# Loads that wait for values, sums begun sooner, and odd chunks on column groups of their own, in a hybrid decoder layer

## The chip, the cores and the metric

The kernel runs on one core of a Trainium2 chip. The time is device microseconds (us) of one execution; a kernel is timed in several runs and the median is taken. One further execution is recorded by the hardware profiler; its trace gives the start and the length of every instruction on TensorE (PE, and PEld for its weight loads), VectorE (DVE), ScalarE (ACT), GpSimd (POOL), on the queue of SyncE (SP), and of every DMA.

## The reference

One decoder layer on x of 1024 tokens by 1024 channels, all in float32:

- h = rmsnorm(x, norm_g) * (1 + scale) + shift, with scale, shift and gate from silu(c) @ w_ada + b_ada
- proj = h @ w_in, cut into q_a, k_a, v_a, z_a (512 wide each: 8 heads of 64) and q_b, f_b, i_b, z_b, g_a, g_b (1024 wide each)
- attention on q_a, k_a, v_a: three dilated causal windows (128 by 1, 512 by 4, 2048 by 16) with a bias by distance, merged by their softmax denominators, then times silu(z_a)
- a gated recurrence on q_b, f_b, i_b, 8 heads of key width 128 and value width 128:

```python
f = lb + (1 - lb) * sigmoid(f_b);  k = 1 - f
S_t = diag(f_t) S_{t-1} + k_t i_t^T;   o_t = S_t^T silu(q_t)
```

- the recurrence's output is normalised and multiplied by silu(z_b); y = sigmoid(g_a) * (o_a @ w_branch_a) + sigmoid(g_b) * (o_b @ w_branch_b)
- out = rmsnorm(x + gate * (y @ w_out), final_g)

## The kernel before

**Products.** A float32 operand is split into a high and a low part (`split`, L243: the high part is a cast on ACT, the low part a subtraction on DVE, helper `sub` at L224). A product of 128 x 128 weights with 128 x 512 of h is then three matmuls (`mm3`, L238 to L241: low times high, high times low, high times high). h is kept transposed as four blocks b11, b12, b21, b22 (halves of the channels by halves of the tokens). Pairs of 128-column units of w_in share their products in Strassen's manner (`add_pair`, L265): seven products on b11, b21, b22 and on the block differences t1 = b12 - b11, t3 = b22 - b12, t2 = b22 - t1, t4 = b21 - t2, instead of eight. The differences are built in place in the tiles xt, by `block_sum` (L667): for each name and each half c of the rows one subtraction on DVE, one cast on ACT (t1h and so on) and one subtraction on DVE (t1l and so on).

**The stream.** All weight products stand in one list of steps (`Stream`, L71). A step's weights are prepared two steps ahead. Raw weight tiles (w_raw) are loaded through SyncE's queue (L258) as soon as a tile of the ring is free; from the thirteenth on, the ring has tiles that take the memory of the start, xt among it. `Filler` (L168) runs pieces of the stream, a group of three matmuls each, between other work: `fill(amount)` owes `amount * rate` groups, about 3.6 for one unit in attention. What leaves PSUM goes through six buffers named ct (`ctile`, L262): products kept for later (L327), and results on their way to DRAM, whose buffer is free again when the write has landed.

**The start (to about 110 us).** x is normalised and turned, h is made block by block (`make_h`, `turn_late`), and the first three units (columns of q, k and v of the first head pair) run along with it (`first_products`, into the banks pm). PE's order is written out by hand in the whole kernel; in the start that of ACT, DVE and GpSimd is too. Between these steps stand calls of `tick` (L680): each begins one more block sum, if one is left, and takes one step of each sum under way.

**Attention (about 110 to 470 us).** For each head, `load_head` (L867) loads the first halves (512 tokens) of q (qp), and of the high and low parts of k (k1, k2), by six loads of 128 KB (`load_half`, L886), a Toeplitz tile of biases (toep, 512 KB, L877) and the values of the first half (`load_value`, vq, L891). All of these go through GpSimd's queue and come from DRAM, where `ev_split` (L428, L429) and the transposes of `ev_v` (L453, vq_d) have put them. The score of 128 queries (`score`, L893) is two matmuls into the bank pss, a sum with toep and a running minimum on DVE (L906), an exp on ACT and two operations on DVE; `turn` (L914) transposes it, and `value` (L929) multiplies it with the values. `begin` (L948) yields after each of the two scores of an item (a head and 256 queries); after the second block of queries (i = 1) it has the second halves and their values loaded, after the last (i = 7) the next head. From the end of the start on, a planner orders the instructions of all engines but PE, loads among them, by when it expects their operands: a load may be issued ahead of its place in the source. So the second halves of head 0 are issued from 89.56 us on, ahead of its first values at 102.11 us.

**The recurrence (about 550 to 950 us).** Each head's 1024 tokens are eight chunks of 128. Within a chunk the decayed products of k and q are built level by level (`recurrence`, L1081): at level hl, blocks of hl keys with the hl queries after them, for hl = 1, 2, 4, 8, 16 by full 32 x 32 tiles (`small`, L1094: output partitions 0, 32, 64 and 96 in turn, so four column groups of the array), for hl = 32 by sixteen products of 32 keys (L1113) and for hl = 64 by eight products of 64 keys (L1122). The output partitions of a matmul are the columns of the array that it uses. ACT copies the results of the last two levels into the matrix am (L1116, L1124), which is needed after all levels. Between the levels DVE updates k and q (L1126, L1128), and the filler runs stream steps.

After 950 us come the branch sums, the output product and the last norm.

Of the kernel before, what the change touches and what calls it, by code (L numbers as in the profile page):

```python
# [10 lines left out]
F32 = mybir.dt.float32  # L11
# [8 lines left out]
P = 128  # L20
S = 1024
# [158 lines left out]
def hybrid_layer(ctx: ExitStack, tc: tile.TileContext, x, w_ada, b_ada, w_in, w_branch_a, w_branch_b, w_out,  # L180
# [203 lines left out]
    def half_of(th):  # L384
        return slice(512 * th, 512 * th + 512)
# [129 lines left out]
    with ExitStack() as st:  # L515
# [113 lines left out]
        def turn_late(j):  # L629

            ps = px.tile([P, 512], F32, name="pxt")
            for t in range(4):
                nc.tensor.transpose(ps[:, t * P:t * P + P], xs[4 + t][:, j * P:(j + 1) * P], ident)
            make_h(j, 1, ps)
# [20 lines left out]
        def first_products(j, ths=(0, 1), us=(0, 1, 2)):  # L655
            for th in ths:
                bh, bl = X[NAMES[j // 4, th]]
                k = j % 4
                for u in us:
                    hi, lo = firsts[u + 3 * (j // 4)]  # L660
                    nc.tensor.matmul(main[u, th], hi[:, k], bh[:, k], start=j == 0, stop=False)
                    nc.tensor.matmul(main[u, th], lo[:, k], bh[:, k], start=False, stop=False)
                for u in us:
                    nc.tensor.matmul(main[u, th], firsts[u + 3 * (j // 4)][0][:, k], bl[:, k], start=False,
                                     stop=j == KT - 1)
# [8 lines left out]
            return [lambda: nc.vector.tensor_tensor(to, a, b_, ALU.subtract),  # L674
                    lambda: nc.scalar.copy(hi[:, s], to), lambda: sub(lo[:, s], to, hi[:, s])]

        sums = [(name, c) for name in ("t1", "t3", "t2", "t4") for c in range(2)]
        under_way = []

        def tick():  # L680

            if sums:
                under_way.append(block_sum(*sums.pop(0)))
            for parts in under_way:
                parts.pop(0)()
            while under_way and not under_way[0]:
                under_way.pop(0)
# [106 lines left out]
        first_products(2, (1,))  # L794
        tick()
        turn_late(3)
        first_products(3, (0,))
        mod_rows(2)
        first_products(3, (1,), (0,))
        mod_turn(2)  # L800
        for n in range(3, 6):
            split_first(n)
        first_products(3, (1,), (1,))
        mod_rows(3)
        first_products(3, (1,), (2,))
        mod_turn(3)
        tick()
        lx.close()
        add_blocks(hctx.enter_context(tc.tile_pool(name="hpool2", bufs=1, reuse_waits="tile")),
                   "b21", "b22", "t2", "t3")  # L810
        stream.issue()
        make_h(4, 0)
        turn_late(4)
        make_h(5, 0)
        first_products(4, (0,))
        turn_late(5)
# [42 lines left out]
    with ExitStack() as at:  # L859
# [7 lines left out]
        def load_head(h):  # L867
            p = h // 2
            if p > 0:
                stream.need(f"qk{p}")  # L870
            while turned.get(("v", p)) != 2:
                stream.step()
            qp, k1, k2 = ([ap1.tile([P, 512], F32R, name=f"{n}{c}") for c in range(2)] for n in ("qp", "k1", "k2"))
            toep = ap1.tile([P, S], F32, name="toep")
            heads[h] = qp, k1, k2, toep, [None, None]
            load_half(h, 0)
            nc.gpsimd.dma_start(toep, bass.AP(tensor=toep_d.tensor, offset=toep_d.offset + h * TOEP,  # L877
                                              ap=[[1, P], [1, S]]))
            load_value(h, 0)

        def load_half(h, c):
            qp, k1, k2, _, _ = heads[h]
            p, r = h // 2, slice(E * (h % 2), E * (h % 2) + E)
            for dst, n in ((qp, 4 * p), (k1, 4 * p + 2), (k2, 4 * p + 3)):
                for hh in range(2):
                    nc.gpsimd.dma_start(dst[c][E * hh:E * hh + E],  # L886
                                        qk_d[n + hh if dst is qp else n][r, half_of(c)].bitcast(F32R))
# [78 lines left out]
                value(*late.pop(0))  # L966

        load_head(0)
        fill.limit = in_gating
        fill.rate = (in_attention - stream.at) * 4 / NH / sum((j + 1) * w for j, w in enumerate(ATT_W))  # L970
        fill(2.0)
        for _ in begin(0):
            fill(0.5)
        for n, (h, j) in enumerate(items):
            nxt = begin(n + 1)
            for m in range(j + 1):
# [61 lines left out]
    with ExitStack() as hg:  # L1038
# [39 lines left out]
        def c3(t):  # L1078
            return t.rearrange("p (c t) -> p c t", c=8)

        def recurrence(h):  # L1081
# [17 lines left out]
            while hl < P:  # L1099
                q4 = qq.rearrange("p (n two t) -> p n two t", two=2, t=hl)  # L1100
                k4 = kk.rearrange("p (n two t) -> p n two t", two=2, t=hl)
                t3 = fq[:, :2 * n].rearrange("p (n two) -> p n two", two=2)
                if hl <= 16:
                    pl = small(2 if hl == 1 else 1)
                    if hl == 1:
                        nc.vector.tensor_tensor(d3, pl[:, :, 0], mask(0), ALU.mult)
                    nc.vector.copy_predicated(d3, mask(1 + LEVELS.index(hl)).bitcast(I32), pl[:, :, 1 if hl == 1 else 0])
                elif hl == 32:
                    pl = pp.tile([P, 512], F32, name="pp")[:, :256]
                    for c in range(8):  # L1110
                        for b in range(2):
                            o = c * P + 64 * b
                            nc.tensor.matmul(pl[64 * b:64 * b + 32, c * 32:c * 32 + 32], kk[:, o:o + 32],  # L1113
                                             qq[:, o + 32:o + 64], start=True, stop=True)
                    for b in range(2):
                        nc.scalar.copy(am[64 * b:64 * b + 32, :, 64 * b + 32:64 * b + 64],  # L1116
                                       c3(pl[64 * b:64 * b + 32]))
                else:
                    pl = pp.tile([P, 512], F32, name="pp")
                    for c in range(8):  # L1120
                        o = c * P
                        nc.tensor.matmul(pl[0:64, c * 64:c * 64 + 64], kk[:, o:o + 64], qq[:, o + 64:o + P],  # L1122
                                         start=True, stop=True)
                    nc.scalar.copy(am[0:64, :, 64:P], c3(pl[0:64]))  # L1124
                k_end = t3[:, :, 1:2].to_broadcast([P, n, hl])
                nc.vector.tensor_tensor(k4[:, :, 0, :], k4[:, :, 0, :], k_end, ALU.mult)  # L1126
                q_end = t3[:, :, 0:1].to_broadcast([P, n, hl])
                nc.vector.tensor_tensor(q4[:, :, 1, :], q4[:, :, 1, :], q_end, ALU.mult)  # L1128
                if fq is tot:
                    tn = g1.tile([P, S // 2], F32, name="totn")  # L1130
                    other = tot, tn
                else:
                    tn = other[0] if fq is other[1] else other[1]
                nc.vector.tensor_tensor(tn[:, :n], t3[:, :, 0], t3[:, :, 1], ALU.mult)
                fq = tn
                n //= 2
                hl *= 2
                yield 2.6
                if hl == 8:
                    load_z(h)  # L1140
                if hl == 32 and h + 1 < NHB:
                    load_f(h + 1)
# [317 lines left out]
```

## Time and profile before

| | |
|---|---|
| three runs | 1139.42, 1141.77, 1144.51 us; median 1141.77 us |
| the profiled execution | 1141.97 us, its span 1140.2 us |
| busy in the span: PE | 1112.2 us (98%), 8322 matmuls |
| PEld | 912.8 us (80%) |
| DVE | 808.2 us (71%) |
| ACT | 516.5 us (45%) |
| POOL | 117.2 us (10%) |
| DMA | 189.54 MB, mean 166 GB/s |
| granted TensorE clock, mean | 0.994 |

The span runs from the first to the last instruction. "Idle before" in a row is the time for which the engine stood still ahead of that instruction, with the instruction or DMA whose end released it. A matmul's end is modelled, and the next one starts before it; the time that a run of matmuls takes is therefore read from start to start.

### The profile page before, as it was taken

Reading aid. Unit: us, or ns where it says so; the run is one execution under the profiler, and the core shown is the slowest. Engines: PE = TensorE matmul, PEld = TensorE weight load, DVE = VectorE, ACT = ScalarE, POOL = GpSimd, SP = SyncE. Lnnn points to the kernel's source line nnn. Section 1 sums busy time; section 2 is a strip of 40 time slices with the busy share of each in tenths; the row PEclk is TensorE's granted clock in tenths of the full one; section 3 lists DMA queues with packets and bytes.
Section 4 is the critical chain, followed back from the end, with each engine's and each line's share of the span. In section 5 each row is a group of like instructions: output and inputs, shape, how many; then the busy total and the mean of one; then the engine's idle time right before and its main releaser. Section 6 shows DMA issues by size and latency. Waiting matters only on the chain.

```text
span 1140.2 us, 21715 instructions
## 1 busy us (share of the span) xinstructions
PE 1112.2 (98%) x8322; PEld 912.8 (80%) x8322; DVE 808.2 (71%) x1607; ACT 516.5 (45%) x1056; POOL 117.2 (10%) x195
## 2 busy tenths in 40 slices
PE   7998999999999999999999999999999999999997
PEld 5677788888888888878887878787887878888886
DVE  4486888878877776844778797878888773769053
ACT  4474555677555555632343444333443432334021
POOL 1102112202202201100000000000000012000000
PEclk9999999999999999999999999999999999999999
DMA  9739476656646624856625254443535379864052
GB/s 321 219 102 252 136 195 181 180 131 163 153 120 162 158 80 139 265 174 195 222 89 173 93 168 140 141 155 107 174 90 181 106 252 328 276 209 140 21 184 74
DMA packets 161480, 189.54 MB, mean 166 GB/s; under 512 B 11312, under 2 KB 107696, under 8 KB 161376
## 3 DMA queue, kind: packets, MB, share of 16 engines
q1 hardware_dynamic: 140080, 153.95, 42.3%
q0 software_dynamic: 20896, 33.60, 12.2%
q8 instruction: 65, 1.06, 0.4%
q10 hardware_dynamic: 400, 0.61, 0.2%
q14 instruction: 39, 0.32, 0.1%
HBM read 129.36 MB, written 58.76 MB: 165 GB/s over the span
## 4 chain that ended last, share of the span: by engine, by line
PE 85%; DVE 6%; DMA 4%; issue 2%; ACT 2%; POOL 1%; SPq 0%; POOLq 0%; DVEq 0%; ACTq 0%
PE m L239 18%; PE m L241 17%; PE m L240 16%; PE pq L240 4%; PE pq L241 4%; PE pq L239 4%; PE po L936 3%; PE pt L921 3%; PE pp L1094 3%; PE pss L904 2%; PE pss L903 1%; PE pou L1177 1%; PE pou L1162 1%; PE pou L1179 1%; PE pxt L640 1%
## 5 line engine op out<-in xcount | busy, mean ns | idle before, releaser
L224 DVE TENSOR_TENSOR w_lo<-w_raw,w_hi 128x512 fp32r<-128x512 f32 x156 | 106.7, 687 | 54.1 <-ACT w_hi L246 48.6
L246 ACT CAST w_hi<-w_raw 128x512 fp32r<-128x512 f32 x146 | 90.5, 620 | 59.9 <-PE m L241 50.3
L327 ACT COPY ct<-m 128x512 f32<-128x512 f32 x90 | 52.6, 585 | 93.7 <-PE m L241 72.0
L246 ACT CAST w_hi<-w_s 128x512 fp32r<-128x512 f32 x90 | 55.9, 621 | 74.0 <-PE m L241 51.0
L274 DVE TENSOR_TENSOR ct<-m,ct 128x512 f32<-128x512 f32 x90 | 61.8, 686 | 26.5 <-PE m L241 26.1
L224 DVE TENSOR_TENSOR w_lo<-w_s,w_hi 128x512 fp32r<-128x512 f32 x90 | 61.8, 687 | 15.2 <-ACT w_hi L246 13.5
L909 ACT ACTIVATE s<-s,st 128x128 f32<-128x128 f32 (+3 forms) x64 | 49.8, 778 | 31.5 <-DVE st L906 31.4
L925 ACT CAST pth<-pt 128x512 fp32r<-128x512 f32 (+1 forms) x80 | 43.6, 544 | 36.5 <-PE pt L921 32.0
L224 DVE TENSOR_TENSOR ptl<-pt,pth 128x512 fp32r<-128x512 f32 (+1 forms) x80 | 50.5, 631 | 7.7 <-ACT pth L925 7.0
L239 PE MATMUL m<-t2h,w_hi 128*128 128x512 f32 x120 | 50.4, 420 | 4.2 <-ACT ct L327 4.2
L1185 POOL TENSOR_TENSOR ssh<-ssh,halfh 128x4 f32<-128x4 f32 x16 | 18.1, 1128 | 345.1 <-DVE ssh L1184 345.1
L239 PE MATMUL m<-b11h,w_hi 128*128 128x512 f32 x124 | 51.6, 416 | 0.0
L239 PE MATMUL m<-b21h,w_hi 128*128 128x512 f32 x124 | 51.2, 413 | 0.0
L239 PE MATMUL m<-b22h,w_hi 128*128 128x512 f32 x124 | 50.8, 410 | 0.0
L239 PE MATMUL m<-t1h,w_hi 128*128 128x512 f32 x120 | 50.3, 419 | 0.5 <-DVE ct L274 0.5
L239 PE MATMUL m<-t4h,w_hi 128*128 128x512 f32 x120 | 49.6, 414 | 0.4 <-DVE ct L274 0.4
L239 PE MATMUL m<-t3h,w_hi 128*128 128x512 f32 x120 | 49.6, 414 | 0.0
L241 PE MATMUL m<-b11l,w_hi 128*128 128x512 f32 x124 | 48.8, 394 | 0.0
L241 PE MATMUL m<-b21l,w_hi 128*128 128x512 f32 x124 | 48.7, 393 | 0.0
L241 PE MATMUL m<-b22l,w_hi 128*128 128x512 f32 x124 | 48.7, 393 | 0.0
L240 PE MATMUL m<-b11h,w_lo 128*128 128x512 f32 x124 | 48.5, 391 | 0.0
L240 PE MATMUL m<-b21h,w_lo 128*128 128x512 f32 x124 | 48.5, 391 | 0.0
(358 smaller groups left out, 3193.8 us busy)
## 6 DMA issues: line engine op xcount, KB each, us to landing
w_raw<-in_w_in_dram SPq DMA_DIRECT2D x128, 256.0 KB, 3.4
wa<-in_w_ada_dram SPq DMA_DIRECT2D x16, 512.0 KB, 8.9
qk_d<-ct SPq DMA_DIRECT2D x32, 256.0 KB, 3.5
k<-qk_d POOLq DMA_DIRECT2D x64, 128.0 KB, 4.9
qp<-qk_d POOLq DMA_DIRECT2D x32, 128.0 KB, 4.9
toep<-toep_d POOLq DMA_DIRECT2D x8, 512.0 KB, 6.5
vq_d<-ct SPq DMA_DIRECT2D x16, 256.0 KB, 3.4
vq<-vq_d POOLq DMA_DIRECT2D x16, 256.0 KB, 4.2
```

What stands on the lines that cost most here:

```text
L224: nc.vector.tensor_tensor(out_, a, hi.bitcast(F32), ALU.subtract)
L239: nc.tensor.matmul(ps, ah, bh, start=start, stop=False, skip_group_check=more)
L240: nc.tensor.matmul(ps, al, bh, start=False, stop=False, skip_group_check=more)
L241: nc.tensor.matmul(ps, ah, bl, start=False, stop=stop, skip_group_check=more)
L246: nc.scalar.copy(hi, src)
L274: nc.vector.tensor_tensor(out_, a, b_, op)
L327: nc.scalar.copy(c[name], b[which])
L909: nc.scalar.activation(s[:, :kw], s[:, :kw], AF.Exp, bias=prev, scale=-1.0, accum_out=st2[:, 2:3])
L921: nc.tensor.transpose(pt[:, c0:c0 + P], pn[b][:, kt * P:(kt + 1) * P], ident)
L925: nc.scalar.copy(pth[:, :w], pt[:, :w])
L936: nc.tensor.matmul(po[:, 256 - n:256], vq[kt // 4][:, kt % 4], src[:, c0:c0 + n], start=kt == 0 and a == 0, stop=kt == 2 * j + 1 and a == 1)
L1094: nc.tensor.matmul(pl[32 * b:32 * b + 32, c], kk[:, o:o + 32], qb[:, 2 - n:2, o:o + 32], start=True, stop=True)
```

## The change

- `sums`: the order of the eight block sums becomes t1, t1, t3, t2, t3, t2, t4, t4.
- `tick` takes an argument: `tick(False)` moves the sums under way by a step and begins none. One more `tick` stands after `turn_late(3)`; the one ahead of `lx.close()` is gone, and `tick(False)` stands after `mod_turn(2)` and after `turn_late(4)`. So both halves of t1 are begun before the second half of h is made.
- `load_half` now loads toep too, half by half (256 KB with each half), ahead of q and k. For the second half of head 0, GpSimd first copies one column of the first value tile into the tiles that are about to be loaded; the loads, which overwrite it, thereby wait until that value tile has landed.
- The first two scores: 2.0 units of filler ran ahead of score block 0 and 0.5 after each of the two; now 0.7 run after block 0 and 2.3 after block 1.
- The recurrence's levels 32 and 64: an odd chunk's products go to output partitions hl further on than those of an even chunk, so that both levels use all column groups in turn. The results lie as four chunk pairs; ACT copies even and odd chunks apart: four copies at hl = 32 (two before) and two at hl = 64 (one before).

```diff
-        sums = [(name, c) for name in ("t1", "t3", "t2", "t4") for c in range(2)]
+        sums = [("t1", 0), ("t1", 1), ("t3", 0), ("t2", 0), ("t3", 1), ("t2", 1), ("t4", 0), ("t4", 1)]
         under_way = []
 
-        def tick():
-
-            if sums:
+        def tick(another=True):
+
+            if sums and another:
                 under_way.append(block_sum(*sums.pop(0)))
             for parts in under_way:
                 parts.pop(0)()
...
         first_products(2, (1,))
         tick()
         turn_late(3)
+        tick()
         first_products(3, (0,))
         mod_rows(2)
         first_products(3, (1,), (0,))
         mod_turn(2)
+        tick(False)
         for n in range(3, 6):
             split_first(n)
         first_products(3, (1,), (1,))
         mod_rows(3)
         first_products(3, (1,), (2,))
         mod_turn(3)
-        tick()
         lx.close()
...
         make_h(4, 0)
         turn_late(4)
+        tick(False)
         make_h(5, 0)
         first_products(4, (0,))
...
             heads[h] = qp, k1, k2, toep, [None, None]
             load_half(h, 0)
-            nc.gpsimd.dma_start(toep, bass.AP(tensor=toep_d.tensor, offset=toep_d.offset + h * TOEP,
-                                              ap=[[1, P], [1, S]]))
             load_value(h, 0)
 
         def load_half(h, c):
-            qp, k1, k2, _, _ = heads[h]
+
+            qp, k1, k2, toep, _ = heads[h]
+            if h == 0 and c == 1:
+                got = heads[h][4][0][:, 0, 0:1].bitcast(F32)
+                for t in (qp[1], k1[1], k2[1]):
+                    nc.gpsimd.tensor_copy(t[:, 0:1], got)
+                nc.gpsimd.tensor_copy(toep[:, 512:513], got)
+            nc.gpsimd.dma_start(toep[:, half_of(c)],
+                                bass.AP(tensor=toep_d.tensor, offset=toep_d.offset + h * TOEP + 512 * c,
+                                        ap=[[1, P], [1, 512]]))
             p, r = h // 2, slice(E * (h % 2), E * (h % 2) + E)
...
         load_head(0)
+        first = begin(0)
         fill.limit = in_gating
         fill.rate = (in_attention - stream.at) * 4 / NH / sum((j + 1) * w for j, w in enumerate(ATT_W))
-        fill(2.0)
-        for _ in begin(0):
-            fill(0.5)
+        for amount in (0.7, 2.3):
+            next(first)
+            fill(amount)
+        next(first, None)
...
-                elif hl == 32:
-                    pl = pp.tile([P, 512], F32, name="pp")[:, :256]
+                else:
+
+                    pl = pp.tile([P, 512], F32, name="pp")[:, :4 * hl].rearrange("p (c t) -> p c t", c=4)
                     for c in range(8):
-                        for b in range(2):
-                            o = c * P + 64 * b
-                            nc.tensor.matmul(pl[64 * b:64 * b + 32, c * 32:c * 32 + 32], kk[:, o:o + 32],
-                                             qq[:, o + 32:o + 64], start=True, stop=True)
-                    for b in range(2):
-                        nc.scalar.copy(am[64 * b:64 * b + 32, :, 64 * b + 32:64 * b + 64],
-                                       c3(pl[64 * b:64 * b + 32]))
-                else:
-                    pl = pp.tile([P, 512], F32, name="pp")
-                    for c in range(8):
-                        o = c * P
-                        nc.tensor.matmul(pl[0:64, c * 64:c * 64 + 64], kk[:, o:o + 64], qq[:, o + 64:o + P],
-                                         start=True, stop=True)
-                    nc.scalar.copy(am[0:64, :, 64:P], c3(pl[0:64]))
+                        for o in range(0, P, 2 * hl):
+                            to = o + hl * (c % 2)
+                            nc.tensor.matmul(pl[to:to + hl, c // 2], kk[:, c * P + o:c * P + o + hl],
+                                             qq[:, c * P + o + hl:c * P + o + 2 * hl], start=True, stop=True)
+                    pairs = am.rearrange("p (c two) t -> p two c t", two=2)
+                    for odd in range(2):
+                        for o in range(0, P, 2 * hl):
+                            nc.scalar.copy(pairs[o:o + hl, odd, :, o + hl:o + 2 * hl],
+                                           pl[o + hl * odd:o + hl * odd + hl])
```

## The prediction

> **What bounds the kernel now.** I read the page first, then busy time by stretches, then what the matmul engine waited for, and last the instructions around each wait in order of time. The profiled execution took 1141.97 us, 1.8 us more than its span and 0.2 us over the median of the three runs (1141.77), so I work against 1141.97 and carry the difference over unchanged.
>
> ```profile
> PE 85%; DVE 6%; DMA 4%; issue 2%; ACT 2%; POOL 1%; SPq 0%; POOLq 0%; DVEq 0%; ACTq 0%
> ```
>
> ```profile
> 90.00:106.00 16.00, 11.84 (x54) 9.65 (x53) 9.26 (x17) 6.80 (x16) 5.00 (x9) 0.89 0.98 221
> 106.00:118.00 12.00, 10.49 (x50) 8.39 (x49) 9.87 (x24) 6.82 (x15) 0.00 (x0) 1.00 1.01 295
> 118.00:460.00 342.00, 341.48 (x1833) 288.49 (x1832) 267.88 (x622) 203.92 (x405) 64.74 (x113) 1.00 0.56 150
> 550.00:950.00 400.00, 396.08 (x4692) 322.44 (x4691) 319.10 (x615) 160.94 (x377) 24.52 (x29) 1.00 0.48 153
> ```
>
> The columns are the stretch, its length, then busy time on PE, weight load, DVE, ACT and POOL, the granted clock, the DMA share and GB/s. PE sets the end: 85% of the chain that ended last is PE, attention (118 to 460) and the recurrence (550 to 950) leave it 0.5 and 3.9 us idle. So a change can win in two ways only: fill a hole in PE's work before 118 us, or make PE's own work shorter.
>
> ```profile
> PE pt L921 <- DVE s L911: 1.5, 2, 1.1
> PE pm L661 <- ACT b21h L652: 1.1, 1, 1.1
> ```
>
> These are two of PE's waits (total us, times, longest) that the edits of the start can reach, for the first softmax rows and for the first block of h's second half; the largest one, 4.16 us for a ct buffer, is shown with part two.
>
> **Part one: the sums begun sooner.** No arithmetic is added; eight sums of three instructions each (DVE, ACT, DVE) only move. In the 1.1 us hole ACT makes a piece of t1 ahead of the h block for which PE waits:
>
> ```profile
> 54.61 0.37 ACT L577 COPY row<-pmod 128x256 f32<-128x256 f32 x1 [2.54 <-PE pmod L574]
> ```
>
> ```profile
> 58.79 1.05 ACT L675 CAST t1h<-xt 128x1024 fp32r<-128x1024 f32 x1
> 59.74 0.81 ACT L651 ACTIVATE xt<-xt,mods 128x512 f32<-128x512 f32 x1
> ```
>
> After the change this cast (1.05 us) lies in the 2.54 us for which ACT stood idle before 54.61, and the second t1 cast between 55 and 56. The h block (L651, for PE's first b21) then starts at 58.79, not 59.74: **0.95 us**. DVE's parts of t1 go the same way, and from 73 us on, where DVE runs without a gap, exactly one of its steps is gone (the t1l below, 1.14 us to the next start; every later tick has as many DVE steps as it had).
>
> ```profile
> 73.24 1.22 DVE L224 TENSOR_TENSOR t1l<-xt,t1h 128x1024 fp32r<-128x1024 f32 x1
> 74.38 1.22 DVE L674 TENSOR_TENSOR xt<-xt 128x1024 f32<-128x1024 f32 x1
> ```
>
> So the last t4l comes 0.95 + 1.14 = 2.1 us sooner. SyncE's queue stands behind it for a w_raw tile, and the first write of the values after that:
>
> ```profile
> SPq L258 <- DVE t4l L224: 7.4, 1, 7.4
> ```
>
> **Part two: the second halves wait.** The big hole:
>
> ```profile
> 96.48 1.03 PE L447 MATMUL pt<-kc,ct 128*128 128x128 f32 x8
> 101.68 0.78 PE L239 MATMUL m<-t2h,w_hi 128*128 128x512 f32 x1 [4.16 <-ACT ct L327]
> ```
>
> ```profile
> 105.20 0.39 PE L241 MATMUL m<-t2l,w_hi 128*128 128x512 f32 x1
> 105.43 0.39 PE L239 MATMUL m<-t2h,w_hi 128*128 128x512 f32 x1
> ```
>
> ```profile
> 101.04 0.59 ACT L327 COPY ct<-m 128x512 f32<-128x512 f32 x1 [4.29 <-DMA vq_d<-ct]
> ```
>
> ```profile
> 94.22 2.30 SPq L453 DMA_DIRECT2D vq_d<-ct  x4
> ```
>
> ```profile
> vq_d<-ct SPq DMA_DIRECT2D x4, 256.0 KB, 6.6
> ```
>
> PE needs its bank copied to a ct buffer; ACT has none until the first write of the values (issued at 94.22) has landed, and these four took 6.6 us where the kernel's median is 3.4:
>
> ```profile
> 90.57 1.59 POOL L886 DMA_DIRECT2D k<-qk_d  x3
> 102.11 0.79 POOL L891 DMA_DIRECT2D vq<-vq_d  x1 [9.95 <-ACT ct L327]
> ```
>
> ```profile
> qp<-qk_d POOLq DMA_DIRECT2D x32, 128.0 KB, 4.9
> ```
>
> ```profile
> vq_d<-ct SPq DMA_DIRECT2D x16, 256.0 KB, 3.4
> vq<-vq_d POOLq DMA_DIRECT2D x16, 256.0 KB, 4.2
> ```
>
> GpSimd put five of the six second-half loads (640 KB; the row shows the last three) into the DMA engines just ahead of it; these, and half of toep (256 KB), leave. At the 221 GB/s of that stretch 0.9 MB are 4.1 us. With the two w_raw loads still ahead, I take a landing of 4.3 us (between 3.4 and 6.6): 94.22 - 2.1 + 4.3 = 96.4, the ACT copy ends 0.6 later, and PE, at the end of its transposes at 97.51 - 0.95 = 96.5, waits to 97.1. Of 4.16 us **3.55** go (with 3.4: all; with 6.6: 1.4). The hole also lowered the granted clock: from 101.68 to 105.20 eight matmul starts take 3.52 us, at 0.23 each 1.8, so **1.7** more go if the hole falls to the size of those between 106 and 118 (1.5 us in all), where the clock stays at 1.00.
>
> The waits: four POOL copies of one column into the tiles of the second half wait for the value tile; behind them stand the seven loads and the other value loads. The copies have no row; one lies between nothing and the small power's 0.73 us:
>
> ```profile
> L599 POOL TENSOR_TENSOR rs<-rs,half 128x1 f32<-128x1 f32 x8 | 5.5, 731 | 20.0 <-DVE rs L598 19.8
> ```
>
> By the clock of before: value load at 102.11, landed 106.3, copies 0 to 2.9, seven issues at 0.55, landing 4.9: 115.1 to 118.0. Row block 4 of head 0 is first to need them:
>
> ```profile
> 124.38 0.49 PE L903 MATMUL pss<-k,qp 128*128 128x512 f32 x1
> ```
>
> Less the 1.7 of clock and the 1.5 below that is 121.2; both sides hang on the same value writes, so the cover of 3 us holds when they come sooner. Cost 0.
>
> **Part three: the first scores sooner.** Score blocks 0 and 1 move ahead of 2.0 units of filler (about 7 groups of three matmuls, 4.8 us).
>
> ```profile
> 111.56 0.22 PE L903 MATMUL pss<-k,qp 128*128 128x128 f32 x1
> ```
>
> PE's two waits for the softmax (1.5 us, the first row of PE's waits) have then 8 groups of cover instead of 2: **1.5 us**. Their loads, issued ahead of the POOL row at 90.57, land by 95.5 at 4.9 us, and block 0 comes at 111.56 - 4.8 - 0.95 - 3.55 - 1.7 = 100.6.
>
> What is late next: over 90 to 118 DVE does 9.26 + 9.87 = 19.1 us, PE 11.84 + 10.49 less 1.7 of slow clock = 20.6. Without the holes DVE would have to run at 93%; in attention it does 78% and PE hardly waits. Holding it to 87% costs 1.4 us, which I take off (between 0 and the 4 that would eat the hole again). Start: 0.95 + 3.55 + 1.7 + 1.5 - 1.4 = **6.3 us**.
>
> **Part four: odd chunks on column groups of their own.** Each head has 16 products of 32 columns (L1113), which so far use two groups of 32, and 8 of 64 columns (L1122), all on the first 64. An f32 product shows as two matmuls. From the first start to the next line's first start:
>
> ```profile
> 560.07 1.10 PE L1094 MATMUL pp<-qb,kk 128*32 128x64 f32 x64
> 561.10 0.50 PE L239 MATMUL m<-t3h,w_hi 128*128 128x512 f32 x1
> ```
>
> ```profile
> 575.00 0.76 PE L1094 MATMUL pp<-qb,kk 128*32 128x32 f32 x64
> 575.70 0.50 PE L239 MATMUL m<-t2h,w_hi 128*128 128x512 f32 x1
> ```
>
> ```profile
> 578.66 0.70 PE L1113 MATMUL pp<-qb,kk 128*32 128x32 f32 x32
> 579.28 0.50 PE L239 MATMUL m<-b22h,w_hi 128*128 128x512 f32 x1
> ```
>
> ```profile
> 581.55 1.15 PE L1122 MATMUL pp<-qb,kk 128*64 128x64 f32 x16
> 582.62 0.50 PE L239 MATMUL m<-b21h,w_hi 128*128 128x512 f32 x1
> ```
>
> L1094 uses four groups: at 32 streamed columns 0.70 / 64 = 10.9 ns each, L1113 on two 0.62 / 32 = 19.4, so the rate goes with the number of groups; on four, 32 x 10.9 = 0.35 us, 0.27 less. At 64 streamed columns four groups take 1.03 / 64 = 16.1 ns, 64 ns within a group; L1122's 67 ns is a group alone, so on two 16 x 33.5 = 0.54, 0.53 less. Eight heads: **6.4 us** (bounds 0 and 6.4). PE sets the pace there, so it counts in full. Evacuation grows:
>
> ```profile
> L1116 ACT COPY amat<-pp 32x256 f32<-32x256 f32 x16 | 5.8, 362 | 5.9 <-PE pp L1113 5.8
> L1124 ACT COPY amat<-pp 64x512 f32<-64x512 f32 x8 | 4.7, 582 | 8.3 <-PE pp L1122 8.3
> ```
>
> These rows give 0.86 ns an element, so four copies of 128 elements are 1.0 us for 0.72 and two of 256 are 0.72 for 0.58: 0.4 us of ACT a head, on an engine busy 161 of 400 us. I charge 0.6 in all for DVE at 80% with less slack: **5.8 us**.
>
> The Trainium skill speaks against this part. "TensorE: Matmul & The Clock Gate", Part 3, "The mechanism", says that weight loads overlap running matmuls only where the row group differs, and here all rows are used; by it part four gains nothing and the sum is 1135.7. The trace disagrees already (10.9 against 67 ns). The same page ("Wait — 56ns, not 53.3ns?") sets a floor of about 25 ns between starts, by which 32 starts would be 0.8 us and L1113 gains nothing; 10.9 ns is far below it.
>
> **Sum.** 6.3 + 5.8 = 12.1; 1141.97 - 12.1 = **1129.9 us**.
>
> **Rivals.** First, the hole moves: ct buffers are still six. The third L327 copy waits again for a value write, and its w_lo is needed about when PE arrives. If that, DVE's load and the second halves (now in flight beside w_raw loads) give back all but 1 us, the time is 1142 - 1 - 5.8 = 1135.2. For it: a DMA share of 1.01 in 106 to 118; against: the 0.9 MB are away when it matters. 0.14.
>
> Second, column groups do not run side by side at 64 columns, or gain nothing at all: 1142 - 6.3 = 1135.7. For it: no row has 64-column tiles on two groups. Against: the four rows above. 0.09.
>
> Third, the change does neither: 1140 to 1142. 0.09.
>
> Fourth, slower: the change of heads. In source order toep's first half now stands ahead of six loads and waits for DVE's last read of the old toep:
>
> ```profile
> 183.71 0.55 POOL L877 DMA_DIRECT2D toep<-toep_d  x1 [0.76 <-DVE st L906]
> ```
>
> ```profile
> 193.91 0.31 PE L903 MATMUL pss<-k,qp 128*128 128x128 f32 x1
> ```
>
> Seven issues from 183.71 end at 187.5, landed at 192.4 by 4.9 us; PE needs them at 193.91. Past a landing of 6.4 us each further us costs seven; past 8.1 us (1.7 over) it eats the whole gain, and 2.3 over gives 1146. Against: the loads are 4.9 us as a rule, and toep has half its size. 0.05.
>
> **Chances and range.** Forecast 0.60 with its own range 1127 to 1134 (best: no remaining wait, no DVE charge, 14.6 off; worst: landing 6.6, clock still lowered); 0.03 lies below it. A measurement here tells about 0.5%, 5.7 us, from no change, so faster is below 1136.1: the forecast, what lies below, and half of the first two rivals: 0.75. Same: the other half and the third, 0.20. Slower 0.05. From 1126 to 1138 takes in the first two rivals.
>
> **What would show it.** Right: PE's first b21 matmul about 1 us sooner; no wait of PE on L327 above 1 us and the granted clock at 1.00 in that stretch; the qp and k second-half loads after the value load; L1113's and L1122's groups at about 0.35 and 0.54 us; a recurrence about 6 us shorter. Wrong: a new PE wait between 97 and 125 us, on w_lo, ct or qp loads; L1122 still at 1.07; waits for pss at the changes of heads.

## The result, and the profile after

The changed kernel takes **1131.62 us** (median of 6 runs, 1130.79 to 1134.09); beside it the kernel before takes 1142.15 (6 runs, 1139.42 to 1144.51). The ratio is 0.9915 with a 95% interval of 0.9903 to 0.9927: 0.85% faster. The forecast was 1129.9. The profiled execution of the changed kernel took 1131.21 us; its page begins, and has as shares of the chain that ended last:

```profile
span 1129.4 us, 21754 instructions
...
PE 86%; DVE 5%; DMA 4%; ACT 2%; issue 2%; POOL 1%; SPq 0%; POOLq 0%; DVEq 0%; ACTq 0%
```

Busy time by stretches, changed kernel, columns as in the prediction:

```profile
90.00:106.00 16.00, 14.87 (x71) 12.19 (x70) 11.16 (x26) 8.32 (x21) 6.52 (x14) 1.00 0.81 218
106.00:118.00 12.00, 12.00 (x59) 9.88 (x59) 10.63 (x25) 7.45 (x18) 1.04 (x2) 1.00 1.15 290
...
550.00:950.00 400.00, 394.79 (x4713) 320.04 (x4712) 320.08 (x620) 165.76 (x404) 26.65 (x32) 1.00 0.49 158
```

Between 90 and 118 us PE is busy 26.9 of 28 us where it was 22.3, and from 90 to 106 the granted clock is 1.00 where it was 0.89. Three of PE's waits in the whole kernel (total us, times, longest):

```profile
PE m L239 <- DVE ct L274: 1.4, 2, 0.9
PE m L239 <- ACT ct L327: 1.1, 1, 1.1
...
PE pss L912 <- DVE st L915: 0.7, 1, 0.7
```

The ct wait fell from 4.16 us to 1.1; the waits for b21h (1.1) and for the softmax (1.5) are gone; a wait for st (0.7) is new, and the one on L274, which lies behind attention, grew from 0.9.

The span is 10.8 us shorter, and four instructions say where. Before, by the timeline (two of them, the ACT copy at 54.61 and the first recurrence product at 560.07, stand in the prediction):

```profile
128.63 0.28 PE L936 MATMUL po<-pth,vq 128*128 128x256 f32 x1
...
955.92 0.39 PE L239 MATMUL pq<-b11h,w_hi 128*128 128x512 f32 x1
```

and the same four after:

```profile
53.83 0.37 ACT L577 COPY row<-pmod 128x256 f32<-128x256 f32 x1 [1.59 <-PE pmod L574]
...
121.87 0.28 PE L945 MATMUL po<-pth,vq 128*128 128x256 f32 x1
...
554.07 1.10 PE L1105 MATMUL pp<-qb,kk 128*32 128x64 f32 x64
...
944.53 0.39 PE L239 MATMUL pq<-b11h,w_hi 128*128 128x512 f32 x1
```

Up to the row copy of L577 the two differ by 0.78 us; no edit reaches PE's work there, and single executions of the other kernels below have this copy anywhere from 52.70 to 54.28, so that is chance. From there to the first value product (call it **A**): 74.02 before, 68.04 after, **6.0 less**. From there to the first product of the recurrence (**B**): 431.44 and 432.20, **0.8 more**. The recurrence, to the first row of the output projections: 395.85 and 390.46, **5.4 less**. Behind it 0.6 are lost. 0.8 + 6.0 - 0.8 + 5.4 - 0.6 = 10.8.

**The start.** The rows that answer to those around the big hole, and the landing of the first four value writes:

```profile
92.48 2.51 SPq L453 DMA_DIRECT2D vq_d<-ct  x4
...
94.80 1.03 PE L447 MATMUL pt<-kc,ct 128*128 128x128 f32 x8
...
96.33 0.58 ACT L327 COPY ct<-m 128x512 f32<-128x512 f32 x1 [1.32 <-DMA vq_d<-ct]
...
96.97 0.50 PE L239 MATMUL m<-t2h,w_hi 128*128 128x512 f32 x1 [1.13 <-ACT ct L327]
...
97.47 0.79 POOL L900 DMA_DIRECT2D vq<-vq_d  x1 [10.02 <-ACT w_hi L246]
...
101.06 0.18 POOL L887 CAST qp<-vq 128x1 fp32r<-128x1 f32 x1 [0.89 <-DMA vq<-vq_d]
...
103.49 2.10 POOL L895 DMA_DIRECT2D k<-qk_d  x4
```

```profile
vq_d<-ct SPq DMA_DIRECT2D x4, 256.0 KB, 3.7
```

The writes are issued 1.74 us sooner, land in 3.7 us instead of 6.6, and the loads of the second halves now come behind the value load and four copies (0.18 us for the first). They are early enough: row block 4, the first to read them, stands at 116.28 (124.38 before) and waits for no load.

**The recurrence.** The groups of head 0 with what follows each on PE, by the timeline:

```profile
572.68 0.46 PE L1125 MATMUL pp<-qb,kk 128*32 128x32 f32 x32
573.07 0.50 PE L239 MATMUL m<-b22h,w_hi 128*128 128x512 f32 x1
...
575.33 0.69 PE L1125 MATMUL pp<-qb,kk 128*64 128x64 f32 x16
575.95 0.50 PE L239 MATMUL m<-b21h,w_hi 128*128 128x512 f32 x1
```

and the copies that empty their banks, in the groups by line and form:

```profile
L1130 ACT COPY amat<-pp 32x128 f32<-32x128 f32 x32 | 8.2, 256 | 5.1 <-PE pp L1125 4.7
L1130 ACT COPY amat<-pp 64x256 f32<-64x256 f32 x16 | 5.9, 368 | 5.6 <-PE pp L1125 5.5
```

Start to start, 32 matmuls take 0.39 us (0.62 before) and 16 take 0.62 (1.07 before): 0.68 a head, 5.4 over eight heads, as the stretch shows.

### The profile page after: what moved, and what is told of

Same layout as the page of the kernel before. It is cut to its first block, busy times and chain, and to the rows that moved or that the text cites. A ratio compares the mean times of both kernels' runs of the same rounds, so it can differ in the third digit from the quotient of the medians.

```text
span 1129.4 us, 21754 instructions
## 1 busy us (share of the span) xinstructions
PE 1104.9 (98%) x8322; PEld 906.1 (80%) x8322; DVE 807.9 (72%) x1607; ACT 519.6 (46%) x1080; POOL 122.3 (11%) x207
## 4 chain that ended last, share of the span: by engine, by line
PE 86%; DVE 5%; DMA 4%; ACT 2%; issue 2%; POOL 1%; SPq 0%; POOLq 0%; DVEq 0%; ACTq 0%
PE m L239 18%; PE m L241 17%; PE m L240 16%; PE pq L240 4%; PE pq L239 4%; PE pq L241 4%; PE po L945 3%; PE pt L930 3%; PE pp L1105 3%; PE pss L913 2%; PE pss L912 1%; PE pou L1184 1%; PE pou L1186 1%; PE pm L661 1%; PE pou L1169 1%
## 5 line engine op out<-in xcount | busy, mean ns | idle before, releaser
L327 ACT COPY ct<-m 128x512 f32<-128x512 f32 x90 | 52.6, 584 | 88.4 <-PE m L241 68.8
L246 ACT CAST w_hi<-w_s 128x512 fp32r<-128x512 f32 x90 | 55.9, 621 | 72.3 <-PE m L241 49.0
L274 DVE TENSOR_TENSOR ct<-m,ct 128x512 f32<-128x512 f32 x90 | 61.8, 687 | 24.8 <-PE m L241 24.3
```

Source lines behind the costliest of these rows:

```text
L246: nc.scalar.copy(hi, src)
L274: nc.vector.tensor_tensor(out_, a, b_, op)
L327: nc.scalar.copy(c[name], b[which])
```

## Experiments

All of them compute the whole of the reference. Parts one to four are those of the prediction: sums, wait, scores, groups. In the table, A and B are the two stretches above from each kernel's own profiled execution, "hole" is PE's wait for the copy of L327 into a ct buffer, "landing" the time from issue to landing of the first value writes. Each ratio is to the kernel before as it ran beside that kernel (medians of 1141.15 to 1142.15 us), so kernels are best compared by their ratios. With the old start (before, e11, e1) the means are 73.8 for A and 431.3 for B; gains and losses of A and B below are against these, or against the change's own profile where a part is left out.

| kernel | median us | ratio to before [95%] | A | B | hole | landing |
|---|---|---|---|---|---|---|
| before | 1142.15 | | 74.0 | 431.4 | 4.16 | 6.6 |
| before, once more (e11) | 1140.08, one run | | 73.5 | 431.0 | 3.78 | 6.1 |
| groups only (e1) | 1135.66 | 0.9947 [0.9930, 0.9964] | 74.0 | 431.5 | 3.09 | 5.5 |
| wait only (e4) | 1142.18 | 1.0003 [0.9989, 1.0016] | 72.7 | 432.5 | 1.56 | 4.0 |
| sums only (e5) | 1140.14 | 0.9991 [0.9975, 1.0006] | 71.8 | 432.5 | 3.11 | 5.5 |
| scores only (e9) | 1140.40 | 0.9984 [0.9972, 0.9996] | 72.3 | 432.9 | 3.39 | 5.4 |
| sums, wait, scores (e2) | 1136.48 | 0.9952 [0.9935, 0.9968] | 67.7 | 432.5 | 1.18 | 3.7 |
| **the change** | 1131.62 | 0.9915 [0.9903, 0.9927] | 68.0 | 432.2 | 1.13 | 3.7 |
| change less wait (e3) | 1134.73 | 0.9929 [0.9908, 0.9950] | 69.3 | 432.2 | 2.21 | 4.8 |
| change less scores (e6) | 1135.19 | 0.9939 [0.9916, 0.9961] | 71.6 | 432.3 | 1.29 | 3.7 |
| change less sums (e10) | 1132.73 | 0.9928 [0.9909, 0.9946] | 69.2 | 433.9 | 1.37 | 3.6 |
| change, all on one group (e7) | 1141.42 | 0.9996 [0.9980, 1.0012] | 67.8 | 432.9 | 1.27 | 3.8 |
| change, first turn at k2 3 (e8) | 1133.07 | 0.9930 [0.9905, 0.9955] | 69.8 | 433.7 | none | 3.1 |

### Part four alone (e1_groups_only)

On the kernel before:

```diff
-                elif hl == 32:
...
+                        for o in range(0, P, 2 * hl):
+                            to = o + hl * (c % 2)
+                            nc.tensor.matmul(pl[to:to + hl, c // 2], kk[:, c * P + o:c * P + o + hl],
+                                             qq[:, c * P + o + hl:c * P + o + 2 * hl], start=True, stop=True)
```

> The kernel before with part four alone (column groups of the recurrence). Theory (the groups run side by side and PE sets the pace, so it counts in full): the two lines take 0.39 and 0.61 us a head as in the changed kernel, 0.62 and 1.07 before, so 8 x 0.69 = 5.5 us less: ratio 0.995, and the start as before with its hole of 4.2 us. Rival (the recurrence gained because the start put the planner's order or the loads in another place): less than 3 us.

0.53% faster, about 6.1 us, with A and B as before. So the recurrence's gain is its own. This profile shows a thing about the start beside it: the hole was 3.09 us and the clock didn't fall behind it, and yet A isn't shorter. PE then waited more for the softmax (1.5 before), and the granted clock fell behind that wait instead, to 0.63 from 114 to 116 us and 0.52 from 116 to 118:

```profile
PE pt L921 <- DVE s L911: 2.5, 2, 1.4
```

### Parts one to three (e2_start_only)

On the changed kernel:

```diff
-                            to = o + hl * (c % 2)
...
+                elif hl == 32:
...
+                            nc.tensor.matmul(pl[64 * b:64 * b + 32, c * 32:c * 32 + 32], kk[:, o:o + 32],
+                                             qq[:, o + 32:o + 64], start=True, stop=True)
```

> The kernel before with parts one to three alone. Theory (the two stages add): the changed kernel's gain less 5.5 us, so 5 to 6 us less than before, the start's trace as in the changed kernel, the recurrence as before. Rival (the start's gain is given back by the recurrence unless that is faster too): less than 3 us.

0.48% faster, about 5.5 us. With e1 the two add up to 1.01%, against 0.85% for the whole; the intervals don't tell these apart. The profiles say the same: the stretch of the recurrence is 390.5 us in e1 and in the change, A is 67.7 here and 68.0 in the change. Nothing shows that the two halves act on each other.

### The change without the wait (e3_no_wait)

```diff
-            if h == 0 and c == 1:
-                got = heads[h][4][0][:, 0, 0:1].bitcast(F32)
-                for t in (qp[1], k1[1], k2[1]):
-                    nc.gpsimd.tensor_copy(t[:, 0:1], got)
-                nc.gpsimd.tensor_copy(toep[:, 512:513], got)
```

> The changed kernel without the four copies that make the second halves wait (toep still in halves). Theory (the second-half loads, put into the DMA engines just ahead, made the value writes land at 6.6 instead of 3.8 us): the wait of PE for the ct copy comes back at 3 to 4 us from 1.1, the clock falls with it or not (0 or 1.7 us): 2.5 to 4.5 us above the changed kernel. Rival (the sums begun 2 us sooner closed the hole, the wait was not needed): under 1 us above it.

The landing is 4.8 us, the hole twice as long, and the clock falls behind it; the timeline and the stretch from 98 to 102 us:

```profile
98.08 0.50 PE L239 MATMUL m<-t2h,w_hi 128*128 128x512 f32 x1 [2.21 <-ACT ct L327]
```

```profile
98.00:102.00 4.00, 3.92 (x12) 3.06 (x13) 2.98 (x6) 2.32 (x8) 2.84 (x4) 0.65 0.68 153
```

A is 1.2 us longer; the medians differ by 3.1, the ratios by 1.6 us with intervals that overlap. The mechanism is shown by the landing and the hole; the price is less sure, 1.2 us in A and 1.6 to 3.1 in the times, mostly below the 2.5 to 4.5 that were expected.

### The wait alone (e4_wait_only)

On the kernel before:

```diff
-            nc.gpsimd.dma_start(toep, bass.AP(tensor=toep_d.tensor, offset=toep_d.offset + h * TOEP,
...
+            if h == 0 and c == 1:
+                got = heads[h][4][0][:, 0, 0:1].bitcast(F32)
...
+            nc.gpsimd.dma_start(toep[:, half_of(c)],
```

> The kernel before with part two alone (toep in halves, second halves wait). Theory: the first value write is issued at 94.2 as before and lands in 3.8 us, so PE waits 1.2 us instead of 4.2 and its clock stays up: 3.0 + 1.7 = 4.7 us less than before, the two softmax waits (1.5 us) stay. Rival (the writes are slow through the w_raw loads ahead of them): the hole stays above 3 us and the gain is under 1.5 us.

No gain at all, though the hole shrank to 1.56 us and the clock stayed at 1.00 behind it: my theory failed here. PE's waits, the rows of the softmax and the stretch behind them show why:

```profile
PE pt L928 <- DVE s L918: 2.8, 2, 1.7
```

```profile
111.10 0.30 PE L928 MATMUL pt<-kc,s 128*128 128x128 f32 x1 [1.66 <-DVE s L918]
...
112.53 0.44 PE L928 MATMUL pt<-kc,s 128*128 128x128 f32 x2 [1.13 <-DVE s L918]
```

```profile
114.00:118.00 4.00, 4.00 (x13) 3.14 (x12) 2.97 (x10) 1.52 (x4) 1.04 (x2) 0.61 1.08 373
```

The softmax waits went from 1.5 to 2.8 us: PE came sooner, DVE didn't. And the fall of the clock wasn't saved, it moved: it came behind these waits. From the transposes at 112.53 to the same place in the work at 117.26 PE takes 4.73 us, where the kernel before takes 3.19 (116.76 to 119.95), so some 1.5 us are lost there, against the 1.7 behind the old hole. Of A only 1.1 us are gained, and B takes back 1.2.

### The sums alone (e5_sums_only)

On the kernel before:

```diff
-        sums = [(name, c) for name in ("t1", "t3", "t2", "t4") for c in range(2)]
+        sums = [("t1", 0), ("t1", 1), ("t3", 0), ("t2", 0), ("t3", 1), ("t2", 1), ("t4", 0), ("t4", 1)]
...
         turn_late(3)
+        tick()
...
         mod_turn(3)
-        tick()
```

> The kernel before with part one alone. Theory: PE's 1.06 us wait for the first b21 is gone (0.95 us), the last t4l and with it the first value write come about 2 us sooner, but the second-half loads are ahead of it as before, so a hole of 2 to 3 us stays and the softmax waits grow to about 2.5 us: 1 to 2.5 us less than before. Rival (the sums alone close the hole): no ct wait above 1.2 us and 4 us less than before or more.

A is 2.1 us shorter (b21h's wait is gone, the hole is 3.11 and the softmax waits are 1.1 where 2.5 had been expected), B is 1.2 longer, and the time falls by 1.0 us, which the interval doesn't tell from nothing.

### The change without the earlier scores (e6_no_early_scores)

```diff
-        for amount in (0.7, 2.3):
-            next(first)
-            fill(amount)
+        fill(2.0)
+        for _ in begin(0):
+            fill(0.5)
```

> The changed kernel without part three (filler of 2.0 units ahead of the first score again). Theory as corrected by the run with the wait alone (where two softmax waits took 2.8 us): PE waits 2.5 to 3 us for the softmax rows, the wait of 0.7 us for a score bank is gone: 1.5 to 2.5 us above the changed kernel. Rival of the prediction (1.5 us of softmax waits against 1.4 us of DVE's overload, which would come with or without the early scores): 0 to 0.5 us above it.

```profile
109.90 0.30 PE L930 MATMUL pt<-kc,s 128*128 128x128 f32 x1 [1.98 <-DVE s L920]
...
111.33 0.69 PE L930 MATMUL pt<-kc,s 128*128 128x128 f32 x2 [1.13 <-DVE s L920]
```

```profile
110.00:114.00 4.00, 2.87 (x9) 2.39 (x10) 3.51 (x9) 2.24 (x6) 0.00 (x0) 0.61 1.21 280
```

With the hole closed and the scores where they were, the softmax waits are 3.1 us in all, the clock falls behind them, and A is 3.5 longer, more than expected. The slow clock is a good part of it: from the transposes at 111.33 to the same place in the work at 114.48 PE takes 3.15 us, where the kernel before takes 1.80 (116.76 to 118.56). By the medians the kernel is 3.6 us over the change, by the ratios 2.7, with intervals that just overlap. The scores are the dearest part to leave out of A, though alone they are worth 1.5 there.

### Both levels on one column group (e7_one_group)

On the changed kernel:

```diff
-                            to = o + hl * (c % 2)
-                            nc.tensor.matmul(pl[to:to + hl, c // 2], kk[:, c * P + o:c * P + o + hl],
...
+                            nc.tensor.matmul(pl[0:hl, c, b], kk[:, o:o + hl], qq[:, o + hl:o + 2 * hl],
```

> The changed kernel with all products of levels 32 and 64 on the first 32 or 64 columns of the array, that is one column group each (evacuation in two copies and one copy, as before the change). Theory (the rate goes with the number of groups, about 39 ns for two matmuls of 32 streamed columns within one group): level 32 takes 32 x 38.8 = 1.24 us, level 64 1.07 us as before, against 0.39 and 0.61: 8 x 1.31 = 10.5 us above the changed kernel. Rival (the rule that weight loads overlap only between row groups, the rate being set by the weight loads): level 32 stays at about 0.62, 8 x 0.69 = 5.5 us above it.

```profile
572.79 1.20 PE L1126 MATMUL pp<-qb,kk 128*32 128x32 f32 x32
573.92 0.50 PE L239 MATMUL m<-b22h,w_hi 128*128 128x512 f32 x1
...
576.18 1.15 PE L1126 MATMUL pp<-qb,kk 128*64 128x64 f32 x16
577.26 0.50 PE L239 MATMUL m<-b21h,w_hi 128*128 128x512 f32 x1
```

By the medians 9.8 us over the changed kernel, by the ratios 9.3. The same 32 matmuls take 1.13 us on one group, 0.62 on two (before) and 0.39 on four; the 16 take 1.08 on one and 0.62 on two. 8 x (0.74 + 0.46) = 9.6. That the groups run side by side is shown, at both widths.

### A later first turn (e8_turn_later)

On the changed kernel, an attempt on the hole that is left: the first value unit's banks are emptied as the later ones' are.

```diff
-    FIRST = ((QA, ev_q(0)), (KA, ev_k(0)), (VA, ev_v(0)))
+    FIRST = ((QA, ev_q(0)), (KA, ev_k(0)), (VA, ev_v(0, 3)))
```

> The changed kernel with the transposes of the first head pair's values one product later, so that the first kept product takes a ct buffer ahead of the four value tiles. Theory (what is left of the hole, 1.1 us, is the ct buffers): PE's wait on the ct copy ahead of the t2 product is gone, about 1 us less than the changed kernel, unless the values come too late for the second halves (needed at 116 us, then landed at about 113). Rival (DVE's load sets the end of this stretch): the 1.1 us reappear as waits between 100 and 125 us and the time is the same.

```profile
PE pt L447 <- DVE ct L224: 1.8, 1, 1.8
PE pss L912 <- DVE st L915: 1.7, 1, 1.7
```

The hole is gone and these two have taken its place, and behind the second of them the granted clock is 0.72 from 122 to 124 us and 0.50 from 124 to 126. By the medians the kernel is 1.5 us over the change, but the intervals overlap. The time in the slow clock lies mostly behind the first value product, so it is part of this kernel's long B.

### The earlier scores alone (e9_scores_only)

On the kernel before:

```diff
-        fill(2.0)
-        for _ in begin(0):
-            fill(0.5)
+        for amount in (0.7, 2.3):
+            next(first)
+            fill(amount)
```

> The kernel before with part three alone. Theory A (the parts of the start cover for each other: a hole that is closed comes back as a softmax wait unless the scores stand earlier, and early scores gain little while the hole stays): the softmax waits (1.1 to 2.8 us in the runs without part three) are gone, the ct hole stays at 3 to 4 us: 0.5 to 2 us less than before. Theory B (part three alone carries the start's gain, since each run without it gave 1 us or less): 4 us less or more.

The softmax waits are gone and A is 1.5 us shorter; the hole is 3.39 and the clock behind it falls:

```profile
99.92 0.80 PE L239 MATMUL m<-t2h,w_hi 128*128 128x512 f32 x1 [3.39 <-ACT ct L327]
```

```profile
102.00:106.00 4.00, 4.00 (x11) 3.14 (x11) 3.14 (x7) 1.54 (x4) 1.21 (x2) 0.56 1.20 255
```

### The change without the sums (e10_no_sums)

On the changed kernel:

```diff
-        sums = [("t1", 0), ("t1", 1), ("t3", 0), ("t2", 0), ("t3", 1), ("t2", 1), ("t4", 0), ("t4", 1)]
+        sums = [(name, c) for name in ("t1", "t3", "t2", "t4") for c in range(2)]
...
-        tick()
...
+        tick()
```

> The changed kernel without part one (sums as before). Theory: the 1.06 us wait for the first b21 is back, the ct wait stays at 1.2 to 1.6 us since the value writes land in 3.8 us, the softmax waits stay away: 1 to 1.5 us above the changed kernel. Rival (the sums' 2 us head start at DVE is what holds the stretch from 100 to 120 us together): 2.5 us above it or more, with waits on DVE there.

1.1 us over the change by medians, inside the intervals. b21h's 1.07 us are back, the hole is 1.37, and B is the longest of all: behind attention PE waits 2.30 us at one place.

```profile
469.73 0.63 ACT L1026 ACTIVATE oar<-oar 128x512 f32<-128x512 f32 x1 [5.16 <-DMA oar<-ga_d]
...
472.34 0.47 PE L239 MATMUL m<-b11h,w_hi 128*128 128x512 f32 x1 [2.30 <-DVE ct L274]
```

### The kernel before once more (e11_before_again)

No edit; to see how far single profiles of one kernel lie apart.

> The kernel before, once more, for the spread of its start between executions. Theory (the size of the hole and of the clock's fall behind it differ from one execution to the next): a ct wait between 3.0 and 4.2 us, a value write that lands in 5 to 7 us, and softmax waits of 1.5 to 2.5 us, the larger the smaller the hole. Rival (the hole is always 4.2 us): the same rows as in the first profile within 0.2 us.

A is 73.5 (74.0 in the first profile), the hole 3.78 (4.16), the landing 6.1 (6.6). So differences in A of half a microsecond between single profiles say nothing; the 1.1 to 6 us above are more than that, though each rests on one profile.

## Why the prediction was right, point by point

The forecast of 1129.9 and its mechanism hold in the main; two terms came out smaller, one partly wrong, and two losses were not in the sum. That the total came within 1.7 us is in part luck, since errors of opposite sign met in part two and in part four. One of the prediction's own signs failed, narrowly: PE still waits 1.13 us on L327, where no wait above 1 us was to be left. And one of its signs of being wrong came in a small way, a new wait before 125 us, of 0.71 us for st.

**Part one: the 0.95 us of the h block hold, the 1.14 behind it do not.** The copy of L577 above now waits 1.59 us instead of 2.54, since the first t1 cast lies in that time, and the h block of L651 starts here:

```profile
58.02 0.81 ACT L651 ACTIVATE xt<-xt,mods 128x512 f32<-128x512 f32 x1
```

That is 1.72 before its old 59.74; less the chance of 0.78, 0.94. The failed step is that a DVE row with one step less ends that step's 1.14 us sooner, so that the value writes come 0.95 + 1.14 = 2.1 us sooner. They came 1.74 sooner, 0.96 without the chance. DVE did lose that step, but two waits of 0.92 us together, which the rows of before don't have, take most of it back:

```profile
75.61 0.69 DVE L224 TENSOR_TENSOR w_lo<-w_raw,w_hi 128x512 fp32r<-128x512 f32 x1 [0.58 <-ACT w_hi L246]
...
82.97 0.69 DVE L224 TENSOR_TENSOR ct<-pm,ct 128x512 fp32r<-128x512 f32 x1 [0.34 <-DMA qk_d<-ct]
```

**Part two: the cause holds, the landing was mis-sized to the good side.** In the table every kernel whose second-half loads go ahead of the value writes has a landing of 4.8 to 6.6 us, every one with the wait 3.1 to 4.0 (forecast 4.3). Without chance PE goes on at 96.97 + 0.78 = 97.75, not at 97.1: the writes were 1.1 later than forecast, the landing 0.6 shorter. So 3.0 of the 4.16 us went instead of 3.55. The clock's 1.7 came too (1.00 behind the hole), but not by part two alone, to which the sum gave it: in e4 the clock fell behind the softmax waits instead, and only where part three has removed these as well does it stay at 1.00 (the change, e2, e7, e10). The wait itself cost nothing: row block 4 waits for no load.

**Part three: 1.5 us, right alone, too small in company.** Alone it takes 1.5 from A, though in that profile the clock is also low for longer (0.56 from 102 to 106, 0.61 before), so the match is not exact; left out of the change it costs 3.5. With the hole closed PE comes to the softmax sooner than DVE does, the waits grow from 1.5 to 3.1, and the clock falls behind them (0.61, e6). The forecast costed each part with the others as they were. Alone the three take 2.1 (sums), 1.1 (wait) and 1.5 (scores) from A, 4.7 in sum; all at once they take 5.8 (the change) to 6.1 (e2) from the same mean.

**The DVE charge of 1.4** was about right. Row block 4 of head 0 comes 8.10 us sooner, 7.3 without chance; the first value product behind it only 6.0. Of these 1.3 some 0.8 lie between the following two rows (4.38 us, 3.54 before), nearly all of it the wait for st (L915). The other 0.5 lie behind the second row, where PE's next score starts at 121.53, just as DVE has read the score before it (121.39 to 121.47). So the place is DVE, as forecast; that the size fits a charge that was chosen and not derived is luck:

```profile
116.28 0.48 PE L912 MATMUL pss<-k,qp 128*128 128x512 f32 x1
...
120.66 0.50 PE L912 MATMUL pss<-k,qp 128*128 128x512 f32 x1 [0.71 <-DVE st L915]
```

Start in all: 6.0 measured, 6.3 forecast.

**Part four: 5.4 us for 6.4.** The step that was off is the rate by division, 32 x 10.9 and 16 x 33.5 ns. Start to start, 64 matmuls on four groups take 0.70 us and 32 take 0.39: 9.7 ns each and some 0.08 us that come once (worked out from these two). That fixed part was divided away. At 64 columns it explains only half of the miss (0.62 for 0.54): (1.07 - 0.08) / 2 + 0.08 is 0.58, and the rest is open. ACT's copies took 1.02 and 0.74 us a head, as forecast; the charge of 0.6 for DVE isn't seen, since 8 x 0.68 already is the stretch's 5.4. The two errors partly cancel: 5.4 net, forecast 5.8.

**Not in the sum: a hole behind attention.** Stretch B is 431.0 to 431.5 us in the three profiles with the old start and 432.2 to 433.9 in all ten with any part of the new one. Most of it is one kind of wait, PE's for the step of L274 that empties its bank into a ct buffer, 0.4 to 0.9 us in all with the old start and 1.4 to 3.0 with any new one; from 460 to 500 us, before and after:

```profile
460.00:500.00 40.00, 39.05 (x173) 31.80 (x172) 29.63 (x48) 23.07 (x42) 3.96 (x8) 1.00 0.67 213
```

```profile
460.00:500.00 40.00, 38.62 (x172) 31.13 (x171) 25.39 (x42) 20.58 (x38) 0.83 (x2) 1.00 0.64 209
```

ACT stands there for a load of ga_d in every kernel, 3.2 to 5.2 us at the longest. Why any new order at the start makes this worse is open; no run here isolates it. It explains in part why the parts of the start look worthless alone: each pays 1.2 to 1.6 us in B for an A that is 1.1 to 2.1 shorter, while all three together pay about the same once.

**The rivals.** "The hole moves" is not what the change does, but it is what part two does by itself (e4: no gain); part three keeps it away. "Column groups do not run side by side" is refuted by e1 and e7. "The change does neither" is refuted by both halves. "The change of heads" did not come: the only pss wait in the list is the 0.7 us of head 0.

## What to carry to other kernels

A hole on the bounding engine is worth what the next wait behind it leaves: before closing it, see which engine PE will meet sooner and give that one its work sooner as well; parts tried one by one can each look worthless (here 0.0, 1.0 and 1.8 us) and be worth 5.5 together. The slow clock behind a hole belongs to this: it can come back behind the next wait, so look at the granted clock all the way to the end of the stretch and not only behind the hole that was closed. A load that nobody needs yet, issued ahead of a write for which somebody waits, can cost that write microseconds (here a landing of 4.8 to 6.6 us instead of 3.1 to 4.0). Small matmuls of one kind gained here, at 32 and at 64 columns, from being spread over the column groups; cost them as a rate plus a fixed part, both from rows of two lengths.

## What the runs showed of the hardware

Column groups work side by side though every tile uses all 128 rows: 35 ns a matmul on one group, 19 on two, 12 on four at 32 columns; 67 and 39 ns at 64 columns. The Trainium skill, "TensorEngine Tiling (Array Packing)", section "Key Properties", says that different tiles can load weights and multiply in parallel, and the traces agree.

The length of a hole alone does not decide whether the granted clock falls behind it. It fell after 4.16, 3.78, 3.39, 3.11 and 2.21 us, and stayed at 1.00 after 3.09 (e1). It fell, too, behind two softmax waits close together (1.39 and 1.13 us in e1, 1.66 and 1.13 in e4, 1.98 and 1.13 in e6) and behind a single wait of 1.71 (e8), but not behind 0.38 and 1.13 (before). The stretch behind the hole in e5 and in e1:

```profile
98.00:102.00 4.00, 2.65 (x8) 2.06 (x9) 2.12 (x4) 2.23 (x6) 2.23 (x4) 0.76 0.42 114
```

```profile
98.00:102.00 4.00, 2.97 (x13) 2.44 (x14) 2.44 (x5) 2.51 (x6) 2.54 (x4) 1.00 0.55 148
```

The Trainium skill, "TensorE: Matmul & The Clock Gate", section "What's actually happening", gives an idle window of about 3.4 us for the fall to half clock. As a limit on the length of a hole that doesn't agree with the 2.21 us of e3 and the 1.71 of e8.
